# Half of a depthwise convolution as diagonal matmuls: a hybrid decoder layer on one core

## The chip, the cores and the metric

One core of a Trainium2 chip runs the whole layer in one launch. The metric is the device time of an execution in microseconds (us); the kernel before has a median of 936.02 us over 3 runs (934.52 to 939.70).

## What is computed

A decoder layer over 1024 tokens of width 1024, in float32. Three mixers read one projection of the normalised input: a gated linear attention (4 heads, chunks), a convolution module, and a causal differential attention (4 heads of 2 x 64). Their outputs are projected, added to x, and a mixture of 16 experts follows. The part that matters here, cut from the reference:

```python
def conv_mixer(u, w, b, gn_g, gn_b):
    a, gt = jnp.split(u, 2, axis=-1)
    z = a * jax.nn.sigmoid(gt)
    zp = jnp.pad(z, ((0, 0), (CONV_WIDTH - 1, 0), (0, 0)))          # CONV_WIDTH = 31
    y = lax.conv_general_dilated(zp, w[:, None, :], (1,), 'VALID',
                                 feature_group_count=CONV_CH) + b   # CONV_CH = 256
    ...                                                             # norm over groups of 64 channels
    return jax.nn.silu(yn)
```

Each of 256 channels is convolved along the tokens with its own 31 weights (taps), the present token and the 30 before it. The 256 channels are two halves of 128, which fill the partitions: ct = 0 and ct = 1.

## The kernel before

**Stages.** In order: norm of x and the projections of the linear attention (to about 97 us); the linear attention in two halves of 512 tokens (`gla_half`); 16 attention steps (4 heads by 4 pairs of token tiles); the output projection; the experts. The order on TensorE is the order of the program text. On VectorE, ScalarE, GpSimd and SyncE a scheduler orders the instructions by its own estimate of when each is ready; each engine then takes its queue strictly in that order.

**Three-pass matmuls.** Float32 operands are split into a high part, rounded to `fp32r`, and the rest (`split`: a copy on ScalarE, L129, and a subtraction on VectorE, L130). A product is the sum of three matmuls, high x high, high x low, low x high (`passes`).

**Filler.** `Filler` holds a queue of generators, each of which yields after every matmul it has issued. `F.fill(n)` lets them issue matmuls with n columns in all at that place in TensorE's order; `F.until(key)` runs the queue until a generator has ended. `gla_half` calls `fill` between the links of its chain: at `GLA_F[2]` to `GLA_F[5]` before and after the levels, `GLA_FILL` matmuls of 256 columns before each of the 7 levels, and `GLA_F[6 + hf]` behind the outputs. A level s (64, 32, ..., 1) is: `keys` on VectorE (L450, L451), the scores `pl` on TensorE (L460), and the scores' way into ST, by ScalarE copies (L469) for 64 and 32 and by two predicated copies on VectorE (L471) from 16 down. The score tiles in PSUM have two buffers, so a level's `pl` waits for the copies of the level before. When ST is complete, `po` (L516, L520) gives the half's output, and ScalarE and VectorE norm it (L524 to L531).

**The convolution.** `conv_proj` (generator "cu", 384 matmuls at L260 with 256 columns) makes z for both halves, and is the filler of the linear attention. `conv_taps` then starts y on ScalarE (L583) and adds one tap per instruction on VectorE, over nearly all 1024 tokens at once (L586); each tap reads and writes y, so the 30 taps of a half follow each other. Two tables, `TAPS[ct]` and `NORMS[ct]`, say how many taps and how many parts of `conv_norm` the program text has in each of the 16 attention steps, both with a priority that lets the scheduler bring them forward to where z is ready.

**Attention.** `head_proj` projects two token tiles per step (L251, 384 columns), brings q, k, v out (`vv`, L129 and L130; `qkr`, `qkss`, L663 to L671), and transposes them (`ptq`, L678). `head_attn` makes scores (L711), maxima (L718), exponentials (L720), transposes and outputs.

## Time and profile before

| | before |
|---|---|
| median of 3 runs | 936.02 us (934.52 to 939.70) |
| profiled execution: its own time / its span | 940.18 us / 938.6 us |
| TensorE matmul busy | 818.2 us (87%), 5256 instructions |
| VectorE busy | 649.2 us (69%), 1441 |
| ScalarE busy | 493.7 us (53%), 1094 |
| GpSimd busy | 165.0 us (18%), 165 |
| mean clock granted to TensorE | 0.931 |

The span runs from the first to the last instruction; the execution's own time is a little longer. In the profile PE is TensorE's matmuls, PEld its weight loads, DVE VectorE, ACT ScalarE. Matmuls are pipelined, so that a matmul's duration is longer than the distance to the next one. A `<-` behind idle time names what ended the wait. The granted clock is in shares of full speed: 1.00 is 2.4 GHz, 0.50 is 1.2 GHz, and a value between is a mean over both. One call of a float32 matmul counts twice in the trace (32 `pl` records are 16 calls).

### The profile page before, as it was taken

What the parts mean: (1) busy time and instruction counts of PE and PEld (TensorE: products, weight loads), DVE (VectorE), ACT (ScalarE), POOL (GpSimd) and SP (SyncE); (2) the same over time, 40 slices, a digit from 0 to 9 for tenths busy, and PEclk for the clock granted to TensorE, in tenths of its full rate; (3) what the DMA queues carried; (4) which work ended last, traced back from release to release, by engine and by line L of the source; (5) the groups of instructions that cost most, each with busy time, mean ns of one, the idle gap of its engine ahead of it and who ended that gap; (6) DMA issues with size and microseconds to landing.
All of it is one profiled execution on the core that took longest, in us unless ns stands there. A gap on an engine that the chain in (4) does not pass through costs nothing. (4 is left out here: it accounts for less than half of the span.)

```text
span 938.6 us, 14319 instructions
## 1 busy us (share of the span) xinstructions
PE 818.2 (87%) x5256; PEld 717.1 (76%) x5256; DVE 649.2 (69%) x1441; ACT 493.7 (53%) x1094; POOL 165.0 (18%) x165
## 2 busy tenths in 40 slices
PE   5999999789768998899878899999399999999870
PEld 4999989688658987788767688888278888888750
DVE  6841556988997666768857666666868677687850
ACT  6743516124246565667757554232558667677730
POOL 5100000000000000000000000000537666664221
PEclk9999989669879999999988999999689999999995
DMA  8210101102002002001202218434479999998942
GB/s 261 76 44 2 46 1 28 37 1 63 6 0 69 1 1 68 1 1 41 68 22 59 81 68 348 168 151 187 170 275 344 335 358 305 363 328 273 318 69 45
DMA packets 46007, 119.29 MB, mean 127 GB/s; under 512 B 6670, under 2 KB 26220, under 8 KB 38636
## 3 DMA queue, kind: packets, MB, share of 16 engines
q0 software_dynamic: 13104, 71.31, 23.0%
q1 hardware_dynamic: 28876, 41.15, 13.2%
q10 hardware_dynamic: 3952, 5.86, 1.7%
q8 instruction: 43, 0.70, 0.3%
q14 instruction: 32, 0.26, 0.1%
HBM read 97.33 MB, written 20.97 MB: 126 GB/s over the span
## 5 line engine op out<-in xcount | busy, mean ns | idle before, releaser
L1272 PE MATMUL pgu<-mw,xT 128*128 128x512 f32 x552 | 140.9, 404 | 0.8 <-ACT xT L129 0.8
L130 DVE TENSOR_TENSOR mw<-mraw,mw 128x1024 fp32r<-128x1024 f32 x99 | 120.9, 1256 | 11.3 <-ACT mw L129 10.4
L1272 PEld LDWEIGHTS pgu<-mw,xT 128*128 128x128 f32 x552 | 102.8, 190 | 24.9 <-issue 1.2
L129 ACT ACTIVATE mw<-mraw 128x1024 fp32r<-128x1024 f32 x113 | 112.9, 1052 | 14.4 <-PE pgu L1272 14.4
L251 PE MATMUL psA<-wh,hnh 128*128 128x384 f32 (+1 forms) x320 | 110.2, 344 | 1.0 <-ACT wh L129 1.0
L251 PE MATMUL psA<-wh,hnl 128*128 128x384 f32 (+1 forms) x320 | 110.6, 346 | 0.2 <-DVE xra L110 0.2
L251 PE MATMUL psA<-wl,hnh 128*128 128x384 f32 (+1 forms) x320 | 109.7, 343 | 0.9 <-DVE wl L130 0.9
L881 PE MATMUL psO<-woh,mx 128*128 128x512 f32 (+1 forms) x272 | 86.8, 396 | 3.5 <-DVE mx L130 2.5
L586 DVE SCALAR_TENSOR_TENSOR mix<-mix,par 128x994 f32<-128x994 f32 (+29 forms) x60 | 75.7, 1262 | 2.1 <-ACT mix L583 1.3
L942 POOL IOTA iota<- 128x128 f32 x1 | 0.2, 238 | 434.9 <-DVE mix L614 434.9
L1300 PE MATMUL py<-mw,hT 128*128 128x512 f32 x276 | 67.3, 392 | 4.5 <-DVE y L1304 2.9
L1300 PEld LDWEIGHTS py<-mw,hT 128*128 128x128 f32 x276 | 51.7, 188 | 16.7 <-ACT hT L129 3.9
L251 PEld LDWEIGHTS psA<-wh,hnh 128*128 128x128 f32 x320 | 63.2, 198 | 1.6 <-ACT wh L129 1.3
L251 PEld LDWEIGHTS psA<-wl,hnh 128*128 128x128 f32 x320 | 63.2, 197 | 1.3 <-DVE wl L130 1.2
L251 PEld LDWEIGHTS psA<-wh,hnl 128*128 128x128 f32 x320 | 63.1, 197 | 0.6 <-DVE hnl L130 0.4
L718 DVE TENSOR_REDUCE nm<-sc 128x1 f32<-128x128 f32 (+7 forms) x64 | 46.8, 751 | 21.7 <-PE sc L714 17.8
L720 ACT ACTIVATE e<-sc,nm 128x128 f32<-128x128 f32 (+7 forms) x64 | 47.3, 740 | 25.6 <-DVE nm L718 21.8
L881 PEld LDWEIGHTS psO<-woh,mx 128*128 128x128 f32 x272 | 49.8, 192 | 12.9 <-DVE mx L130 2.9
L260 PE MATMUL psA<-hnh,wl 128*128 128x256 f32 x192 | 57.1, 297 | 0.0
L260 PE MATMUL psA<-hnl,wh 128*128 128x256 f32 x192 | 57.0, 297 | 0.0
L260 PE MATMUL psA<-hnh,wh 128*128 128x256 f32 x192 | 56.1, 292 | 0.2 <-DVE mix L556 0.2
L881 PE MATMUL psO<-wol,mx 128*128 128x512 f32 (+1 forms) x136 | 53.5, 394 | 0.0
(388 smaller groups left out, 1841.8 us busy)
## 6 DMA issues: line engine op xcount, KB each, us to landing
mraw<-in_expert_w_gate_dram POOLq DMA_DIRECT2D x15, 1024.0 KB, 9.1
mraw<-in_expert_w_up_dram POOLq DMA_DIRECT2D x15, 1024.0 KB, 10.2
mraw<-in_expert_w_down_dram POOLq DMA_DIRECT2D x15, 1024.0 KB, 15.2
wraw<-in_w_in_dram SPq DMA_DIRECT2D x64, 128.0 KB
mix<-in_x_dram SPq DMA_DIRECT2D x8, 512.0 KB
wraw<-in_w_out_dram SPq DMA_DIRECT2D x16, 256.0 KB
h<-in_x_dram SPq DMA_DIRECT2D x8, 512.0 KB
out_dram<-h SPq DMA_DIRECT2D x8, 512.0 KB
```

The costliest lines, as they stand in the source:

```text
L129: K.nc.scalar.activation(hi, src, AF.Copy)
L130: (eng or K.nc.vector).tensor_tensor(lo, src, hi.bitcast(FT), op=OP.subtract)
L251: nc.tensor.matmul(ps[:, :n], a[:, k, cs], b[:, k % 2, :n], start=(k == 0 and t == 0), stop=(k == KT - 1 and t == 2))
L260: nc.tensor.matmul(ps, a[:, k % 2, c0:c0 + 128], b[:, k, :], start=(k == 0 and t == 0), stop=(k == KT - 1 and t == 2))
L586: nc.vector.scalar_tensor_tensor(y[:, sh:], z[:, :S - sh], w(t), y[:, sh:], op0=OP.mult, op1=OP.add)
L718: nc.vector.tensor_reduce(nm, scs[m][:, :n], axis=AX.X, op=OP.max, negate=True)
L720: nc.scalar.activation(e[:, :n], scs[m][:, :n], AF.Exp, bias=nm, accum_out=sums[:, u, m:m + 1])
L881: nc.tensor.matmul(ps, a[:, k, :], b[:, k % 4, c0 % 512:c0 % 512 + c1 - c0], start=(k == 0 and t == 0), stop=(k == KT - 1 and t == 2))
L942: g.iota(t, allow_small_or_imprecise_dtypes=True, **kw)
L1272: nc.tensor.matmul(ps, a[:, k, :], b[:, k % 4].rearrange("p a f -> p (a f)"), start=(n == 0), stop=(n == 23))
L1300: nc.tensor.matmul(py[:, c * 512:(c + 1) * 512], a[:, k, :], b[:, k, c * 512:(c + 1) * 512], start=(k == 0 and t == 0), stop=(k == 1 and t ...
```

## The change

The first channel half (ct = 0) leaves `conv_taps`. A new generator `conv_mm`, queued as "cv" behind "cu", computes it on TensorE: for each of the 31 taps a 128 x 128 matrix with the channels' weights on its diagonal, against z shifted by the tap, summed in one PSUM tile per column half of 512 tokens. With the three passes these are 31 x 3 x 2 = 186 matmuls of 512 columns (`pcv`, L616 of the new file). The diagonals (`dg`) are made on ScalarE from the identity with a scale per partition (L614): a high and a low one per tap and column half, 124 in all, with three buffers each. z is split once per column half (`dz`), with one buffer each. The fills of `gla_half` are made larger, and `F.until("cv")` ends the generator before the attention. `TAPS[0]` becomes empty, `TAPS[1]` and `NORMS[0]` are spread over other steps, and the pool of the norm's gain row is closed early, to give its room to the new tiles.

```diff
-GLA_FILL = 6
+GLA_FILL = 16
...
-TAPS = [[6, 6, 6, 6, 4, 2, 0, 0, 0, 0, 0, 0, 0, 0, 0, 0], [0, 0, 0, 0, 4, 4, 5, 5, 5, 4, 3, 0, 0, 0, 0, 0]]
-NORMS = [[0, 0, 0, 0, 0, 0, 0, 2, 0, 1, 1, 0, 0, 0, 0, 0], [0, 0, 0, 0, 0, 0, 0, 0, 0, 0, 0, 1, 2, 1, 0, 0]]
+TAPS = [[0] * 16, [3] * 10 + [0] * 6]
+NORMS = [[0, 0, 1, 0, 1, 0, 1, 1, 0, 0, 0, 0, 0, 0, 0, 0], [0, 0, 0, 0, 0, 0, 0, 0, 0, 0, 0, 1, 2, 1, 0, 0]]
...
-GLA_F = [40, 32, 16, 12, 10, 10, 44, 102]
+GLA_F = [40, 32, 24, 20, 16, 16, 60, 150]
...
+def conv_mm(K, dp, ct):
+    nc = K.nc
+    W = 31
+    y, z = K.mix[:, 2 + ct, :], K.z[:, ct, :]
+    wh = dp.tile([128, W], FT, name="dwh")
+    wr = dp.tile([128, W], FR, name="dwr")
+    wl = dp.tile([128, W], FT, name="dwl")
+    wv = K.par[:, R_CW:R_CW + 2 * W].rearrange("p (t c) -> p t c", c=2)[:, :, ct]
+    nc.scalar.activation(wr, wv, AF.Copy)
+    nc.scalar.activation(wh, wr.bitcast(FT), AF.Copy)
+    nc.vector.tensor_tensor(wl, wv, wh, op=OP.subtract)
+    for hf in range(2):
+        zs = [dp.tile([128, W - 1 + 512], FR, name=f"dz{x}") for x in range(2)]
+        lo = hf * 512 - (W - 1)
+        if hf == 0:
+            for t in zs:
+                nc.scalar.activation(t[:, :W - 1], K.ident[:, :W - 1], AF.Copy, scale=0.0)
+            split(K, zs[0][:, W - 1:], zs[1][:, W - 1:], z[:, :512])
+        else:
+            split(K, zs[0], zs[1], z[:, lo:lo + W - 1 + 512])
+        ps = K.psum.tile([128, 512], FT, name="pcv", tag="acc", bufs=2)
+        for t in range(W):
+            d = [dp.tile([128, 128], FR, name=f"dg{x}", bufs=3) for x in range(2)]
+            for x, wt in enumerate((wh, wl)):
+                nc.scalar.activation(d[x], K.ident, AF.Copy, scale=wt[:, t:t + 1])
+            for m, (a, b) in enumerate(passes(d, zs)):
+                nc.tensor.matmul(ps, a, b[:, t:t + 512], start=(t == 0 and m == 0), stop=(t == W - 1 and m == 2))
+                yield 512
+        nc.scalar.activation(y[:, hf * 512:hf * 512 + 512], ps, AF.Identity,
+                             bias=K.par[:, R_CBIAS + ct:R_CBIAS + ct + 1])
...
-    K.rowp = pool(K, sg, "rowp")
+    sr = ExitStack()
+    K.rowp = pool(K, sr, "rowp")
...
+    sr.close()
+    dp = pool(K, sg, "convd")
     F.add("cu", conv_proj(K, cp))
+    F.add("cv", conv_mm(K, dp, 0))
...
     gla_half(K, gp, 1, st, F)
+    F.until("cv")
     sg.close()
...
-    F.until("cu")
-    conv = [conv_taps(K, cp, ct) for ct in range(2)]
+    conv = [iter(()), conv_taps(K, cp, 1)]
```

**How the order moves.** VectorE in the last levels of the linear attention's second half, before (the taps, L586, are those of ct = 0; `lm_980` and `lm_986` are levels 2 and 1):

```order
L451 TENSOR_TENSOR kq<-mix,dex 128x256
L586 SCALAR_TENSOR_TENSOR mix<-mix,par 128x1001
L586 SCALAR_TENSOR_TENSOR mix<-mix,par 128x1002
L471 COPY_PREDICATED ST<-lm_980,pl 128x256x2
L586 SCALAR_TENSOR_TENSOR mix<-mix,par 128x1003
L471 COPY_PREDICATED ST<-lm_980,pl 128x256x2
L586 SCALAR_TENSOR_TENSOR mix<-mix,par 128x1004
L586 SCALAR_TENSOR_TENSOR mix<-mix,par 128x1005
L586 SCALAR_TENSOR_TENSOR mix<-mix,par 128x1006
L586 SCALAR_TENSOR_TENSOR mix<-mix,par 128x1007
L586 SCALAR_TENSOR_TENSOR mix<-mix,par 128x1008
L471 COPY_PREDICATED ST<-lm_986,pl 128x512 x2
```

The same place in the changed kernel; the taps are now those of ct = 1:

```order
L450 TENSOR_TENSOR kq<-mix,dex 128x256
L451 TENSOR_TENSOR kq<-mix,dex 128x256
L586 SCALAR_TENSOR_TENSOR mix<-mix,par 128x994
L586 SCALAR_TENSOR_TENSOR mix<-mix,par 128x995
L586 SCALAR_TENSOR_TENSOR mix<-mix,par 128x996
L471 COPY_PREDICATED ST<-lm_980,pl 128x256x2 x2
L586 SCALAR_TENSOR_TENSOR mix<-mix,par 128x997
L586 SCALAR_TENSOR_TENSOR mix<-mix,par 128x998
L586 SCALAR_TENSOR_TENSOR mix<-mix,par 128x999
L471 COPY_PREDICATED ST<-lm_986,pl 128x512
L586 SCALAR_TENSOR_TENSOR mix<-mix,par 128x1000
L471 COPY_PREDICATED ST<-lm_986,pl 128x512
```

Fifteen taps of ct = 0 stood ahead of the last copy into ST, the first of them behind the copies of level 16; now seven of ct = 1 stand there, the first behind the copies of level 4.

TensorE in the changed kernel around level 4 of that half (`pl` are a level's scores, `pcv` the new matmuls; before, the filler at each of these places was six matmuls of `conv_proj`):

```order
L460 MATMUL pl<-kq 128x64 x16
L414 MATMUL pdec<-gU,mix 128x128 x4
L616 MATMUL pcv<-dz_2275,dg_2283 128x512
L616 MATMUL pcv<-dz_2275,dg_2319 128x512
L616 MATMUL pcv<-dz_2276,dg_2319 128x512
L616 MATMUL pcv<-dz_2275,dg_2320 128x512
L616 MATMUL pcv<-dz_2275,dg_2326 128x512
L616 MATMUL pcv<-dz_2276,dg_2326 128x512
L616 MATMUL pcv<-dz_2275,dg_2327 128x512
L616 MATMUL pcv<-dz_2275,dg_2333 128x512
L460 MATMUL pl<-kq 128x64 x16
```

From here on the new matmuls take the place of `conv_proj`'s, which has ended by then; 26 of them stand ahead of the last `po`, 75 and 85 behind it.

VectorE where the first head's projection begins, before (`vv`, `qkss` and `qka` are the first head's; the taps are those of ct = 1):

```order
L586 SCALAR_TENSOR_TENSOR mix<-mix,par 128x1000
L130 TENSOR_TENSOR vv<-psA,vv 128x128
L586 SCALAR_TENSOR_TENSOR mix<-mix,par 128x1001
L667 TENSOR_REDUCE qkss<-qksq 128x4
L586 SCALAR_TENSOR_TENSOR mix<-mix,par 128x1002
L107 TENSOR_SCALAR qkv<-qkss 128x8
```

The same place in the changed kernel (L699 is the former L667):

```order
L586 SCALAR_TENSOR_TENSOR mix<-mix,par 128x1022
L586 SCALAR_TENSOR_TENSOR mix<-mix,par 128x1023
L130 TENSOR_TENSOR vv<-psA,vv 128x128
L699 TENSOR_REDUCE qkss<-qksq 128x4
L130 TENSOR_TENSOR vv<-psA,vv 128x128
L699 TENSOR_REDUCE qkss<-qksq 128x4
L107 TENSOR_SCALAR qkv<-qkss 128x8
```

Before, the taps of ct = 1 alternated with the first head's operations; now the last of them stands ahead of the first `vv`.

## Rows read from the trace of the kernel before

**Rows 1.** The page's slices (40 equal ones): TensorE's granted clock in tenths.
```profile
PEclk9999989669879999999988999999689999999995
```

**Rows 2.** Windows: stretch, length; busy PE, PEld, DVE, ACT, POOL (count); clock; DMA; GB/s.
```profile
97.00:145.20 48.20, 45.54 (x498) 42.82 (x497) 27.98 (x48) 18.04 (x40) 0.00 (x0) 0.93 0.09 23
145.20:168.30 23.10, 23.04 (x275) 22.00 (x276) 15.23 (x28) 13.61 (x27) 0.00 (x0) 1.00 0.18 48
168.30:204.20 35.90, 26.39 (x175) 23.75 (x174) 35.10 (x35) 3.25 (x7) 0.00 (x0) 0.54 0.04 12
204.20:224.80 20.60, 20.60 (x169) 20.60 (x170) 16.41 (x22) 9.34 (x21) 0.00 (x0) 0.97 0.00 1
224.80:252.40 27.60, 19.28 (x102) 18.12 (x100) 25.66 (x35) 7.39 (x18) 0.00 (x0) 0.88 0.22 58
252.40:286.70 34.30, 25.91 (x153) 22.65 (x152) 31.46 (x71) 14.73 (x50) 0.00 (x0) 0.85 0.00 1
...
329.50:355.00 25.50, 23.42 (x161) 20.77 (x160) 16.14 (x54) 15.82 (x54) 0.00 (x0) 1.00 0.01 2
```

**Rows 3.** The same windows, line 586 (the taps) alone: VectorE's busy time.
```profile
168.30:204.20 35.90, 27.31 (x22) 0.54 0.04 12
...
224.80:252.40 27.60, 19.81 (x16) 0.88 0.22 58
252.40:286.70 34.30, 18.06 (x15) 0.85 0.00 1
```

**Rows 4.** Waits of TensorE, 97 to 290 us: total us, times, longest.
```profile
PE pl L460 <- DVE ST L471: 8.4, 6, 2.0
...
PE ptq L678 <- DVE qkr L671: 6.4, 1, 6.4
PE po L516 <- DVE ST L471: 3.0, 1, 3.0
```

**Rows 5.** Timeline of TensorE, 729.8 to 734 us: start, us, instruction.
```profile
730.72 2.98 PE L1272 MATMUL pgu<-mw,xT 128*128 128x512 f32 x12
733.54 0.39 PE L1284 MATMUL pth<-ident,sg 128*128 128x128 f32 x2
```

**Rows 6.** Timeline of VectorE, 170 to 195 us: keys, three taps, two copies into ST.
```profile
172.74 0.42 DVE L450 TENSOR_TENSOR kq<-mix,dex 128x256 f32<-128x256 f32 x1
...
173.41 3.84 DVE L586 SCALAR_TENSOR_TENSOR mix<-mix,par 128x997 f32<-128x997 f32 x3
...
192.34 2.43 DVE L471 COPY_PREDICATED ST<-lm,pl 128x512 f32<-128x512 int32 x2
194.56 1.24 DVE L586 SCALAR_TENSOR_TENSOR mix<-mix,par 128x1009 f32<-128x1009 f32 x1
```

**Rows 7.** Timeline of TensorE: a level's scores and the outputs, first half and second half.
```profile
109.07 1.12 PE L460 MATMUL pl<-kq 32*128 32x64 f32 x32
...
134.20 1.00 PE L520 MATMUL po<-mix,ST 128*128 128x64 f32 x8
...
135.53 1.00 PE L520 MATMUL po<-mix,ST 128*128 128x64 f32 x8
...
171.12 2.57 PE L460 MATMUL pl<-kq 32*128 32x64 f32 x32 [1.99 <-DVE ST L471]
...
194.69 1.81 PE L520 MATMUL po<-mix,ST 128*128 128x64 f32 x8
...
197.25 1.81 PE L520 MATMUL po<-mix,ST 128*128 128x64 f32 x8
```

**Rows 8.** Timelines of ScalarE and VectorE: the split of a 512-column operand.
```profile
157.24 0.62 ACT L129 ACTIVATE wh<-wraw 128x512 fp32r<-128x512 f32 x1
...
158.59 0.68 DVE L130 TENSOR_TENSOR wl<-wraw,wh 128x512 fp32r<-128x512 f32 x1
```

**Rows 9.** ScalarE with a scale per partition, 128 columns: durations of L806, and a pair.
```profile
L806 ACT ACTIVATE on<-on,osa x32: 385/394/435, 279.8 to 567.4; 128x128 f32<-128x128 f32 x32
...
316.09 0.70 ACT L806 ACTIVATE on<-on,osa 128x128 f32<-128x128 f32 x2 [0.62 <-DVE osa L803]
```

## The prediction

> **What bounds the kernel now.** I read the page's slices first. The clock granted to TensorE falls to six tenths in the eighth and ninth of the 40 slices (164 to 211 us) and to eight and seven in the eleventh and twelfth (235 to 282) [rows 1]: the second half of the linear attention, and the entry of the attention. The windows cut this part into stages [rows 2]. The first half of the linear attention (97 to 145.2) and the start of the second (to 168.3) are TensorE's: busy 23.04 of 23.10 us at full clock. Then, from 168.3 to 204.2, VectorE is busy 35.10 of 35.90 us, TensorE only 26.39, at a mean clock of 0.54. At the entry of the attention it is the same: VectorE 25.66 of 27.60 and 31.46 of 34.30 us, TensorE 19.28 and 25.91.
>
> The same windows for line 586 alone say why: 22 taps of the convolution, 27.31 us, lie in the 35.9 us stretch, 16 and 15 in the two after it [rows 3]. The waits name the price on TensorE: 8.4 us of `pl` and 3.0 us of `po` behind VectorE's writes of ST, 6.4 us of a transpose behind `qkr` [rows 4]. So taps that sit in VectorE's queue between links of the chains for TensorE cost TensorE's time; TensorE is the bound elsewhere in these stages.
>
> **The change, part by part.** The sum is made on TensorE's queue from 97 us to the scores of the third attention step (286.7 us), since behind it no tap is left and the work is the same.
>
> *Taken away: TensorE's waits in the linear attention.* 8.4 + 3.0 = 11.4 us [rows 4].
>
> *Taken away: the half clock there.* A mean clock of 0.54 over 35.9 us is 33 us at half rate. TensorE was idle about 9.5 us of that stretch, so some 24 us of work ran at half rate and cost 12. The clocks of 0.93 over 48.2 us and 0.97 over 20.6 us add 2.4 and 0.6 [rows 2]. Together 15.0 us.
>
> *Taken away: the taps at the entry of the attention.* In the new order all 30 taps of the second channel half stand ahead of the first `vv`. They run while TensorE works off the rest of the diagonal matmuls, 160 of them, some 38 us, and 23 x 1.28 us of taps fit into that. The stretch of the first two steps, 34.3 us, should then be like that of the first two steps of the second head, 25.5 us at clock 1.00 [rows 2]: 8.8 us. The stretch before it, 27.6 us, holds 19.28 us of TensorE work at clock 0.88; without half rate this is about 17.5 us, and nothing waits for long: 10.1 us. Together 18.9 us. In sum 11.4 + 15.0 + 18.9 = 45.3 us go.
>
> *Added: 186 matmuls with 512 columns* (31 taps, 3 passes, 2 halves). Twelve such matmuls start at 730.72 and what follows at 733.54, so one takes 2.82 / 12 = 0.235 us [rows 5]: 43.7 us. The Trainium skill (TensorE: Matmul & The Clock Gate, section "Wait — 56ns, not 53.3ns?") gives 215.7 ns from start to start for 512 columns at full clock. By it the sum would be 3.6 us lower; the trace here shows 0.235, and I stay with that.
>
> The fills are larger too, but move conv_proj's 384 matmuls only forward; that costs nothing, because the count on TensorE's queue is the same. They are used up before the last levels of the second half. There the filler is 26 of the new matmuls, and 160 are left behind `po`.
>
> *Added: a new wait in the last levels.* The diff says the taps leave VectorE, but only the first half's do. The order shows the other half's taps moving up into their place: 3 before the write of ST for level 2, 3 before that for level 1 and one between its two parts, where 15 stood before. From the write of level 4 VectorE needs: keys 0.67 us, 3 taps 3.84, ST 2.22, 3 taps 3.84, then ST 2.22 with a tap of 1.24 in it, together 14.0 us [rows 6]. TensorE has in that time two score groups of 1.12 us [rows 7] and 16 new matmuls of 0.235: 6.0 us. So it waits about 8.0 us.
>
> *Added: half clock behind that wait.* Before, a wait of 1.99 us was followed by scores that took 2.57 us for 1.12, and the outputs `po` then took 2.56 us per group where the first half's took 1.33 [rows 7]. I take half rate for the four groups of `po`: 4 x 1.23 = 4.9 us. The bounds are nothing, and twice that if the diagonal matmuls behind also begin at half rate.
>
> *Added: the seam between the two column halves.* The pieces of z exist once, so the second half's split waits for the first half's last matmul, behind the evacuation on ScalarE: two operations on 512 columns there at 0.62 us, then one of 0.68 us on VectorE [rows 8], and I add 0.5 us for the ends between the three engines: 2.4 us. Between nothing and 5 if the clock falls.
>
> *Added on ScalarE: 124 diagonals.* The nearest row is a 128 x 128 activation with a scale per row: two in 0.70 us, 0.394 for one, so the second starts 0.31 us after the first [rows 9]. A tap takes 0.62 us of ScalarE and 0.705 of TensorE, and three buffers run ahead, so TensorE stays the bound and the price is nothing. The upper end is 0.394 with no overlap: 0.79 us a tap, 53 taps x 0.08 = 4.5 us, and with ScalarE's other work in that tail (on, two mix, two evacuations, a split: some 5.5 us) about 10 us. The three first pairs of diagonals, ahead of 97 us, lie where ScalarE waits for TensorE.
>
> *Moved:* the norms of the first half come at steps 2 to 7 instead of 7 to 10, same count: nothing, as VectorE has room there (16.14 of 25.5 us) [rows 2]. The loads on SyncE keep their order; the weight splits of the first head now stand before the tail.
>
> **The sum:** 43.7 + 8.0 + 4.9 + 2.4 - 45.3 = +13.7 us on the profiled execution of 940.18 us. That one is 4.2 us above the median of the runs, 936.0; on the median I forecast **950 us**, slower by 1.5%. By itself this case reaches from 944 to 956.
>
> **Rivals.**
> *1. ScalarE bounds the tail.* For it: 106 diagonals follow each other there, each waiting for a buffer that TensorE frees. Against it: the pair in 0.70 us. It decides from 0.35 us a diagonal; price 10 us, with a clock that falls in the small gaps up to 16: 960 to 966 us.
>
> *2. The clock comes back during `po`.* In the first half `po` went from half to full rate within one burst (its later groups 1.33 us); in the second half 10 us of it stayed at half [rows 7]. If the new matmuls before it keep the rate up, 4.9 us fall away: 945 us. The Trainium skill (TensorE: Matmul & The Clock Gate, "What's actually happening") speaks for this: half rate is the resting state and sustained activity releases it. The second half's `po` here did not follow that.
>
> *3. The last levels are not held, the other side.* If the taps run in the shadow of TensorE's own work, the 8.0 and 4.9 us are not paid: +0.8 us, 937. The place is the pair of writes of ST at levels 2 and 1; the point is 1.6 us of new waits in all (45.3 - 43.7): under it the kernel is faster. With no seam and 512 / 2.4 GHz = 0.213 us a matmul (39.7 us), 39.7 - 45.3 = -5.6: 930 us. Against it: VectorE takes its queue in order, and 14.0 us of work cannot hide behind 6.0.
>
> *4. The change doesn't relieve the attention's entry.* If the taps of the second half are still running when the first head's `vv` come, up to 18.9 us stay: 969 us. Against it: the tail is as long as the taps.
>
> **How the numbers follow.** The forecast 0.45, rival 1 0.18, rival 2 0.14, rival 3 0.19, rival 4 0.04. Range 934 to 966: it leaves out rival 4 and the far end of rival 3. Of this kernel a measurement can tell about 0.5%, 4.7 us, from no change. Faster by more is half of rival 3: 0.10. Within 0.5%: the other half of it, with the lower edges of the forecast and of rival 2: 0.17. Slower: 0.73.
>
> **What would show it.** Right: about 186 matmuls `pcv` at 0.235 us with TensorE near full in a tail of some 42 us between `po` and the first attention projection; waits of `pl` and `po` behind ST of some 8 us in the second half; no wait of a transpose behind `qkr`; the third step's scores some 14 us later than 286.7. Wrong: `pcv` waiting for ScalarE (rival 1), a clock near 1 in the second half's `po` (2), no waits behind ST there (3), taps beside the first head (4). If the scores of the third step come at 287 or earlier, the sum has failed on the side of the gains.

## The result, and the profile after

The changed kernel takes 943.84 us (median of 15 runs, 941.19 to 948.67). Beside it the kernel before took 939.7 us (15 runs). The ratio is 1.0051, with a 95% interval of 1.0033 to 1.007: slower by 0.5%, some 4 us, where the forecast had +13.7 and 1.5%. The direction was right, the size was not. The forecast's 950 also stood on the median of three runs, 936.0; on 939.7 the same sum would have been 953.4.

The profiled execution took 948.67 us (span 947.0), 8.4 us more in span than the one of before. The slices of the page, against [rows 1]: of the low clock in the sixth, eighth, ninth, eleventh and twelfth slices only eight tenths in the ninth are left; behind that it's there about as before, in the 23rd slice (seven tenths) instead of the 22nd, and in the 29th and 30th (seven and seven instead of six and eight).

```profile
PEclk9999999989999999999989799999779999999995
```

The windows of the same stages (columns as in [rows 2]):

```profile
96.50:145.20 48.70, 48.47 (x550) 46.39 (x549) 27.00 (x47) 20.77 (x45) 0.00 (x0) 1.00 0.14 37
145.20:169.10 23.90, 23.56 (x193) 22.99 (x191) 14.07 (x24) 11.09 (x25) 0.00 (x0) 1.00 0.13 34
169.10:210.10 41.00, 36.14 (x392) 31.65 (x392) 30.84 (x41) 17.71 (x40) 0.00 (x0) 0.92 0.16 40
210.10:252.50 42.40, 40.28 (x169) 31.83 (x169) 28.35 (x28) 36.95 (x108) 0.00 (x0) 0.96 0.00 1
252.50:295.08 42.58, 40.56 (x256) 37.14 (x255) 21.07 (x70) 19.64 (x66) 0.00 (x0) 1.00 0.00 1
```

The third line is the second half of the linear attention, the fourth the tail of diagonal matmuls (42.4 us, forecast 42), the fifth the attention's entry. The entry takes 42.6 us where the last two stretches before it took 61.9 [rows 2]. The third step's scores start at 295.08, 8.35 us later than before.

The new wait, in TensorE's timeline (start, us, instruction, idle time before it and what ended it):

```profile
191.06 0.44 PE L460 MATMUL pl<-kq 32*128 32x64 f32 x4 [0.83 <-DVE ST L471]
...
197.25 0.44 PE L460 MATMUL pl<-kq 32*128 32x64 f32 x4 [2.45 <-DVE ST L471]
198.39 1.97 PE L460 MATMUL pl<-kq 32*128 32x64 f32 x28 [0.69 <-DVE ST L471]
200.29 3.78 PE L616 MATMUL pcv<-dz,dg 128*128 128x512 f32 x8
203.87 1.04 PE L516 MATMUL po<-stlast,qb 128*128 128x256 f32 x2
...
205.45 0.66 PE L520 MATMUL po<-mix,ST 128*128 128x64 f32 x4 [0.15 <-DVE ST L471]
```

and VectorE's queue that makes it:

```profile
190.30 1.29 DVE L471 COPY_PREDICATED ST<-lm,pl 128x512 f32<-128x512 int32 x2
...
192.16 3.83 DVE L586 SCALAR_TENSOR_TENSOR mix<-mix,par 128x994 f32<-128x994 f32 x3
195.91 2.42 DVE L471 COPY_PREDICATED ST<-lm,pl 128x512 f32<-128x512 int32 x2
198.13 3.82 DVE L586 SCALAR_TENSOR_TENSOR mix<-mix,par 128x997 f32<-128x997 f32 x3
...
204.10 1.29 DVE L471 COPY_PREDICATED ST<-lm,pl 128x512 f32<-128x512 int32 x1
```

This is the forecast's chain: 190.30 to 205.39, 15.1 us (forecast 14.0). TensorE's waits on ST in it are 4.3 us, not 8.0, because its work was slowed meanwhile: the last scores take 1.97 for 1.12, eight `pcv` 3.78 for 1.9. Waits and slow work together are 7.1 us. Then `po` came back to full rate: a group of it takes 2.08 us at first, then 1.32.

The diagonal matmuls and their diagonals, by line:

```profile
L616 PE MATMUL pcv<-dz,dg x186: 387/395/795, 184.8 to 252.2; 128*128 128x512 f32 x186
L614 ACT ACTIVATE dg<-ident,dwh x62: 384/402/405, 71.7 to 250.4; 128x128 fp32r<-128x128 f32 x62
```

From 232.62 the last 85 take 19.8 us to the next instruction: 0.233 us each, against 0.235 in [rows 5]. The second line is the high diagonals; the 62 low ones (`dwl`) run beside them. ScalarE waits 10.7 us for TensorE to free diagonals, 7.8 of it ahead of the tail. In the tail it is busy 18.0 of 19 us (233 to 252), so it keeps up with little to spare; that it doesn't set the pace is shown by e3 below.

### The profile page after: what moved, and what is told of

It is laid out like the page before. It is cut to its first block, busy times and chain, and to the rows that moved or that the text cites. A ratio compares the mean times of both kernels' runs of the same rounds, so it can differ in the third digit from the quotient of the medians.

```text
span 947.0 us, 14847 instructions
## 1 busy us (share of the span) xinstructions
PE 849.0 (90%) x5442; PEld 740.8 (78%) x5442; DVE 620.5 (66%) x1414; ACT 535.2 (57%) x1225; POOL 162.3 (17%) x165
## 5 line engine op out<-in xcount | busy, mean ns | idle before, releaser
L1332 PE MATMUL py<-mw,hT 128*128 128x512 f32 x276 | 68.9, 399 | 3.5 <-DVE y L1336 2.2
L260 PE MATMUL psA<-hnh,wl 128*128 128x256 f32 x192 | 55.0, 286 | 0.0
L260 PE MATMUL psA<-hnl,wh 128*128 128x256 f32 x192 | 54.6, 285 | 0.0
L616 PE MATMUL pcv<-dz,dg 128*128 128x512 f32 x186 | 48.7, 418 | 2.7 <-ACT dz L129 1.4
```

Source lines behind the costliest of these rows:

```text
L260: nc.tensor.matmul(ps, a[:, k % 2, c0:c0 + 128], b[:, k, :], start=(k == 0 and t == 0), stop=(k == KT - 1 and t == 2))
L616: nc.tensor.matmul(ps, a, b[:, t:t + 512], start=(t == 0 and m == 0), stop=(t == W - 1 and m == 2))
L1332: nc.tensor.matmul(py[:, c * 512:(c + 1) * 512], a[:, k, :], b[:, k, c * 512:(c + 1) * 512], start=(k == 0 and t == 0), stop=(k == 1 and t ...
```

## The experiments

All times in one table. "Scores" is the start of the third step's scores in the profile, "to projection" the time from there until the fourth head is ready for its first output projection, "mx" TensorE's waits in that projection. The last four columns come from the timelines of each profile, so from one execution each; the first two from all runs of the comparison. The three profiles of the changed kernel differ by 5.0 us in "scores" and 2.2 in "to projection": smaller differences in these columns show little by themselves.

| kernel | median us (runs) | ratio to before, interval | scores | to projection | mx | span |
|---|---|---|---|---|---|---|
| before | 939.7 (15) | | 286.7 | 229.1 | 3.5 | 938.6 |
| before, again | 940.54 (1) | | 287.6 | 228.4 | 3.4 | 938.9 |
| changed | 943.84 (15) | 1.0051, 1.0033 to 1.007 | 295.1 | 223.0 | 7.7 | 947.0 |
| changed, again | 945.87 (6) | 1.0049, 1.0025 to 1.0072 | 300.0 | 222.0 | 7.3 | 946.2 |
| changed, third | 948.78 (1) | | 296.5 | 220.8 | 7.4 | 947.1 |
| e1: gate | 942.61 (12) | 1.0014, 0.9984 to 1.0044 | 292.8 | 222.8 | 7.4 | 942.3 |
| e10: filler | 947.16 (12) | 1.0087, 1.0057 to 1.0117 | 297.7 | 220.4 | 5.0 | 944.4 |
| e11: gate, filler | 938.31 (10) | 0.9982, 0.9959 to 1.0005 | 290.4 | 220.6 | 8.3 | 938.7 |
| e13: gate, late | 944.48 (12) | 1.0037, 1.0012 to 1.0063 | 295.5 | 218.8 | 7.7 | 942.2 |
| e3: two passes | 939.1 (10) | 0.9983, 0.9962 to 1.0004 | 294.8 | 221.2 | 2.9 | 937.2 |
| e5: before, fills | 943.07 (10) | 1.0035, 1.001 to 1.0061 | 290.6 | 225.6 | 3.1 | 942.6 |
| e8: before, gate | 935.15 (10) | 0.9957, 0.9932 to 0.9981 | 283.3 | 227.3 | 2.8 | 933.6 |
| e15: norms back | 947.9 (10) | 1.0077, 1.0042 to 1.0111 | 293.0 | 225.4 | 7.8 | 945.7 |
| e16: weights | 933.37 (7) | 0.9929, 0.9891 to 0.9966 | 300.8 | 220.7 | 1.0 | 937.1 |
| e18: before, weights | 931.77 (7) | 0.9919, 0.9887 to 0.9951 | 287.9 | 226.4 | 0.5 | 928.3 |
| e14: split | 929.36 (6) | 0.989, 0.9851 to 0.9929 | 284.5 | 225.8 | 2.7 | 930.1 |
| e17: split, norms | 923.62 (6) | 0.9821, 0.9782 to 0.9861 | 280.6 | 218.8 | 2.7 | 917.6 |
| e19: all | 915.87 (6) | 0.977, 0.9728 to 0.9812 | 279.7 | 218.5 | 0.5 | 909.5 |

### More profiles of the two kernels

No edit.

> The changed kernel as it is, for a second profile. The first one had a span of 947.0 us, 8.4 longer than the kernel before, where the medians differ by 4.1; behind the third step's scores the two traces take the same 651.9 us. Theory A (the four outputs po are not slowed by the clock in this kernel, and the rest of what the forecast missed is the spread of single executions): again po in about 6.2 us at full rate behind waits of the scores on VectorE of some 3 to 4 us, third step's scores at 295 give or take 1, and a span between 940 and 948 that goes with the granted clock behind them. Theory B (the profile caught po in a lucky phase): po takes some 10 us at half rate in this one, and the third step's scores come at 299.

> The kernel before as it is, for a second profile. In the first one the third step's scores start at 286.7 and what follows takes 651.9 us; the changed kernel's two profiles have 295.1 and 300.1, and 651.9 and 646.2 behind. Theory A (the part behind the third step varies by some 6 us from one execution to the next in both kernels alike, with the clock in the attention's fourth head and at the first experts): third step's scores again at 286 to 288, and between 645 and 653 us behind them. Theory B (the part behind is shorter in the changed kernel by its own doing, and that is why the medians differ by 4 while the stage differs by 8 to 13): again about 652 behind.

> The changed kernel as it is, for a third profile. Theory A: the third step's scores between 295 and 300, by the clock in po of the second half (full or half rate), and between 645 and 652 us behind them. Theory B (the part behind is shorter in the changed kernel by its own doing): about 646 behind; 651.9 in the first profile was the exception.

In the second profile `po` of the second half runs at half rate after waits of 4.0 us, so the scores come at 300.0; in the third it comes back to full rate in its first group, 296.5. In the second profile `po` takes 10.8 us where it took 6.0 (203.9 to 209.9) in the first, and TensorE's timeline shows where the waits fell, with the window behind it:

```profile
199.38 1.11 PE L460 MATMUL pl<-kq 32*128 32x64 f32 x28 [0.44 <-DVE ST L471]
...
204.20 0.70 PE L516 MATMUL po<-stlast,qb 128*128 128x256 f32 x2 [1.65 <-DVE ST L471]
...
206.43 1.12 PE L520 MATMUL po<-mix,ST 128*128 128x64 f32 x4 [1.14 <-DVE ST L471]
```

```profile
204.20:215.20 11.00, 9.86 (x41) 9.13 (x42) 9.52 (x8) 0.00 (x0) 0.00 (x0) 0.57 0.00 0
```

So both cases of the forecast's clock term occur in one and the same program. They differ in where TensorE waits for VectorE: in the first profile the last scores ran slowly (1.97 us), TensorE came to `po` late and waited 0.15 us there; in the second they ran at full rate (1.11), TensorE came early, waited 2.8 us at `po` itself, and half rate followed. In the third it waited nothing there. The other profiles say the same: wherever TensorE waited 1.1 us or more at the second half's `po` (both of before, e3, e4, e5, e10, e16, e18), its later groups took 2.2 to 2.6 us (in e5 1.9, then 1.3), and wherever it waited under 0.5 us, they took 1.3. Behind the scores 651.9, 646.2 and 650.6 us follow, against 651.9 and 651.3 before: neither theory, but a sum of two things that differ in the table, "to projection" and "mx".

### The last levels: gate and filler

e1 keeps every tap behind the last copy into ST; e10 has no gate, but more filler ahead of the last levels; e11 has both; e13 gates and spreads `conv_proj` so that it lasts until `po`.

```diff
+                K.gla_st = nc.vector.copy_predicated(...).ins
...
-                    if GATE and ct == 0:
-                        with tc.issue_after(K.gla_last):
+                    if ct == 1:
+                        with tc.issue_after(K.gla_st):
```

```diff
-        F.fill(GLA_FILL * 256)
+        F.fill((GLA_FILL if hf == 0 or li < 5 else [28, 36][li - 5]) * 256)
...
-    F.fill(GLA_F[5] * 256)
+    F.fill((GLA_F[5] if hf == 0 else 40) * 256)
```

e11 has [24, 28] and 24 there. e13 has 6 a level and GLA_F of before in the first half, and 16, 16, 20, 24, 32, 36, 36 and 32 in the second.

> The second channel half's taps on VectorE all stand behind the last write of ST, so none lies between the links of the last levels; otherwise the changed kernel. Theory A (the taps ahead of the writes of ST at levels 2 and 1 hold the scores, and the half clock follows from that): the stretch from level 4's scores to po, 16.6 us in the changed kernel, takes 7.8 us; the 30 taps run beside the diagonal matmuls behind po (30 x 1.28 = 38 us from about 196, so they end at 239 to 241, just before the attention starts at about 244): 8.8 us less, 935 us, faster than both kernels. Rival B (what the levels gain the attention's entry gives back, since the taps now end too late): vv and qkr wait, the entry takes over 42.6 us, 940 to 944. Rival C (the half clock there comes from something else than the wait): scores still take 1.97 us for 1.12, and only the waits of 3.4 us go: 940.

> The changed kernel with 32 of its 186 diagonal matmuls in place of 24 as filler between the last levels and po: 14, 18 and 20 ahead of level 2, level 1 and po of the second half, where 8 each stood, so 28 fewer are left behind po; nothing else moves. Theory A (the waits behind ST at levels 2 and 1 cost twice, by themselves and by the half clock that follows; filler costs nothing, since it only moves): the waits on ST of 4.3 us in the first profile and 4.0 in the second go, and with them the half clock from level 1 to po, 2.8 us in the first and some 8 in the second: third step's scores at 287 to 289 instead of 295 and 300, 944 - 7 = 937 or less. Rival B (the clock falls there without any wait, as it did in the kernel with the taps gated, where 1.5 us of waits were left): scores still take 1.97 us for 1.12, only the waits go, third step's scores at 292, 940. Rival C (what is gained ahead of the third step is lost behind it, as between the first two profiles of the changed kernel): third step's scores at 288, but 944 all the same.

> The kernel whose second half's taps stand behind the last write of ST, with 12, 14 and 12 diagonal matmuls as filler ahead of level 2, level 1 and po of the second half, where 8 each stood. Theory A (1.5 us of waits at level 2 bring the half clock there, and filler takes both away): no wait on ST over 0.3 us, level 1's scores in 1.12 us, third step's scores at 287 to 289 instead of 292.8, about 937. Rival B (the clock falls without a wait): scores at 1.6 to 1.97 us again, third step's scores at 291.5, 941.

> The kernel whose second half's taps stand behind the last write of ST, with the fills of the first half as before the change (6 a level), and those of the second half's levels larger (16 to 36 units of 256 columns), so that conv_proj's matmuls last until po and all 186 diagonal matmuls stand behind po. Theory A (the diagonals come late from ScalarE at levels 4 to 1, 0.6 to 1.9 us of waits of pcv there, and with the waits behind ST they bring the half clock; conv_proj's matmuls need no diagonals): no wait over 0.3 us between 168 and po, scores in 1.12 us, po at full rate, the 186 in 43.7 us with the seam: third step's scores at 284 to 287 instead of 290.4 of the gated kernel with more filler, about 933. Rival B (the clock falls in the last levels without a wait): scores of levels 2 and 1 at 1.6 to 1.97 us, 938. Rival C (the taps end too late: 30 x 1.28 = 38 us from about 203, with conv_proj's writes and the weight splits between them to 245 or later, as the tail ends): waits at vv and qkr, 940.

*e1*: the waits on ST fall to 1.0 us, but level 2 and the `pcv` behind it still run at half rate and level 1 partly: rival C's clock, and only 2.3 us of the 8.8 show in this one profile. The taps, ending at 244, cost the entry nothing (42.6 us), against rival B. *e10* (14, 18 and 20 matmuls are 52 in place of 24; the 32 in its text is a slip) is slower than the changed kernel. VectorE's queue there:

```profile
192.79 5.12 DVE L586 SCALAR_TENSOR_TENSOR mix<-mix,par 128x994 f32<-128x994 f32 x4
197.83 2.46 DVE L471 COPY_PREDICATED ST<-lm,pl 128x512 f32<-128x512 int32 x2
200.09 7.72 DVE L586 SCALAR_TENSOR_TENSOR mix<-mix,par 128x998 f32<-128x998 f32 x6
207.72 2.43 DVE L471 COPY_PREDICATED ST<-lm,pl 128x512 f32<-128x512 int32 x2
```

The room that the filler makes is taken by more taps, 4 and 6 instead of 3 and 3: the last copy ends at 210.2, `po` waits 2.7 us and runs at half rate. None of my three theories had that. *e11*, with the gate as well, has no wait on ST and gains 5.5 us on the changed kernel; its scores come at 290.4. What is left are 1.9 us of waits for diagonals and half rate behind them. *e13* has no such wait and no half rate from 166 to 203.7 (clock 1.00), yet its scores come at 295.5: its first half, with the small fills, runs at 0.95 over 68.9 us with waits again, and 186 matmuls in one piece take 49.2 us with seam and waits. Filler is moved, not made.

### The price and the gain by themselves

e3 leaves out the third pass, e4 the whole convolution of the first channel half but one tap.

```diff
-            for m, (a, b) in enumerate(passes(d, zs)):
+            for m, (a, b) in enumerate(passes(d, zs)[:2]):
```

```diff
 def conv_mm(K, dp, ct):
...
+    nc.scalar.activation(y, z, AF.Identity, scale=w, bias=...)
+    return
+    yield
```

> Leaves out one of the three passes of the diagonal matmuls (the low part of the weights, so 124 matmuls instead of 186; both diagonals per tap are still written). Theory A (TensorE bounds the tail and the price of the change is 0.235 us a matmul): up to 62 x 0.235 = 14.6 us less, 929 us, but only as long as ScalarE keeps up. Theory B (ScalarE's two diagonals at 0.30 us each are right under TensorE's three passes at 0.70): a tap falls from 0.70 to 0.60 us and no further, 53 x 0.10 + 9 x 0.235 = 7.4 us less, 936.5, with pcv waiting for the diagonals all through the tail. Theory C (ScalarE bounds the tail already in the changed kernel): no change, 944.

> Leaves out the first channel half's convolution but for one tap, which is one operation on ScalarE: no diagonals, no diagonal matmuls, so what taking the taps off VectorE is worth without the price on TensorE. Theory A (the gain is about 40 to 45 us, and the diagonal matmuls cost their full count): 160 matmuls behind the last levels x 0.235 = 37.6 and the seam of 2.1 go, 904 us; the filler of the last levels ran beside waits and gives nothing. Rival B (the tail of diagonal matmuls is also the cover of the second half's taps: without it some 20 taps, 26 us, stand ahead of the first vv): 8 to 19 us come back at the attention's entry, 912 to 923, with vv or qkr waited for there. Rival C (the taps of the first half cost little before): less than 25 us under the changed kernel, 919 or more, and no wait at the attention's entry.

*e3*: the scores come at 294.8, no earlier than with all 186. In it the low diagonals are still written, but nothing reads them, so no buffer holds them back: all 62 are done by about 102 us, and in the tail ScalarE writes one diagonal per tap.

```profile
L614 ACT ACTIVATE dg<-ident,dwl x62: 386/390/400, 73.4 to 102.2; 128x128 fp32r<-128x128 f32 x62
```

So theory B, two diagonals per tap as the limit, isn't put to the test here. Behind `po` the first nine `pcv` start about 0.43 us apart at a low clock, then they follow each other at 0.233 us:

```profile
222.00:226.20 4.20, 4.20 (x12) 3.33 (x12) 3.05 (x4) 2.63 (x5) 0.00 (x0) 0.55 0.00 0
226.30:232.20 5.90, 5.90 (x26) 4.52 (x24) 3.62 (x8) 5.23 (x15) 0.00 (x0) 1.00 0.00 0
```

That is the pace of the changed kernel's tail too, with two diagonals per tap: TensorE sets it, not ScalarE. From the end of `po` to the attention e3 takes 30.2 us instead of 42.6, as theory A's price has it (62 x 0.233 = 14.4, less what half rate took of it). But ahead of that TensorE waits longer (10 us, for diagonals and for ST), as twelve taps stand ahead of the last copy into ST instead of seven, and `po` runs at half rate: what the tail gains is lost there. The median's 5 us come from behind: `mx` is waited for 2.9 us instead of 7.4. *e4*: without a convolution the routing is another (576 matmuls `pgu` instead of 552), so its 948.03 us say nothing and only the stage counts: scores at 274.2, 21 to 26 us earlier than with the 186, not 40. The waits of TensorE there, from its timeline:

```profile
207.87 1.22 PE L516 MATMUL po<-stlast,qb 128*128 128x256 f32 x2 [5.44 <-DVE ST L471]
229.12 1.94 PE L537 MATMUL pt<-ident,ong 128*128 128x128 f32 x8 [10.74 <-DVE ong L531]
```

Rival B, at another place than it said: not the attention but the gate output `ong` stands behind the taps. With `pl` TensorE waits 25.3 us there for VectorE, against 4.3 in the first profile of the changed kernel. So the diagonal matmuls (43 us) partly run in time that TensorE would have waited, and taking the taps off VectorE, in this order and with the larger fills, is worth 13 us (287.2 to 274.2).

### The kernel before with one part of the change

e5 has the larger fills alone, e8 the gate alone (both channel halves).

```diff
-GLA_FILL = 6
+GLA_FILL = 16
...
-GLA_F = [40, 32, 16, 12, 10, 10, 44, 102]
+GLA_F = [40, 32, 24, 20, 16, 16, 60, 150]
```

> The kernel before with the larger fills of the change alone: 60 taps on VectorE, no diagonal matmuls. Theory A (the fills alone give nothing; conv_proj's matmuls run out ahead of the last levels, where the waits on ST then have no filler at all): waits of pl and po behind ST of 15 us or more instead of 11.4, third step's scores at 288 to 292, 940 to 945. Rival B (earlier filler is worth something by itself, as the first half's waits go): third step's scores at 283, 936.

> The kernel before with all 60 taps behind the last write of ST: nothing leaves VectorE, the taps only move out of the last levels. Theory A (VectorE bounds this whole part: 92.2 of 97.8 us busy from 168 to 266 in the kernel before; what the levels gain, the entry of the attention loses): no waits on ST, po some 15 us earlier, then waits of the attention's transposes on qkr or vv of 10 us and more, third step's scores at 284 to 290, 938 to 943. Rival B (the waits and the half clock at the levels were the whole loss, and moving the taps is enough): third step's scores at 272 to 278, 928, and the diagonal matmuls not needed.

*e5* follows theory A: waits of 17.1 us of `pl` and 5.4 of `po` behind ST. *e8* is the surprise: nothing leaves VectorE, the taps only wait for the last copy, and the kernel is 0.4% faster than before. TensorE's waits from 168 to 284 us, longest last:

```profile
PE ptq L678 <- DVE qkr L671: 10.1, 1, 10.1
PE pa L739 <- DVE e L726: 9.4, 3, 4.9
...
PE pl L460 <- DVE ST L471: 1.2, 2, 0.7
```

Against [rows 4], `po` has none left and `pl` little, and `qkr` 10.1 instead of 6.4: theory A's exchange, a little better than even.

### Behind the third step

VectorE in the changed kernel at the fourth head, and ScalarE (ACTq is its queue):

```profile
515.84 1.76 ACTq L874 DMA_DIRECT2D wr<-in_router_expert_w_dram  x1
```

```profile
523.44 0.36 DVE L875 TENSOR_TENSOR wr<-wr,par 128x192 f32<-128x192 f32 x1 [4.30 <-DMA wr<-in_router_expert_w_dram]
...
525.25 1.22 DVE L130 TENSOR_TENSOR mx<-mix,mx 128x1024 fp32r<-128x1024 f32 x1
```

```profile
526.53 0.79 PE L913 MATMUL psO<-woh,mx 128*128 128x512 f32 x1 [5.56 <-DVE mx L130]
```

VectorE waits 4.30 us for the router weights, which nobody needs yet, with `mx` behind them in its queue, and TensorE waits 5.56 for `mx`. In the kernel before the issue took 0.60 us and the same place reads:

```profile
513.54 0.60 ACTq L842 DMA_DIRECT2D wr<-in_router_expert_w_dram  x1
```

```profile
520.01 1.22 PE L881 MATMUL psO<-woh,mx 128*128 128x512 f32 x2 [2.50 <-DVE mx L130]
```

e15 puts the table of the first half's norms back; e16 and e18 issue the two loads of the router weights from GpSimd, in the changed kernel and in the kernel before. VectorE's scaling of them then stands behind both parts of `mx`.

```diff
-NORMS = [[0, 0, 1, 0, 1, 0, 1, 1, 0, ...
+NORMS = [[0, 0, 0, 0, 0, 0, 0, 2, 0, 1, 1, ...
```

```diff
-    nc.scalar.dma_start(wr[:, :, :4], ...
+    nc.gpsimd.dma_start(wr[:, :, :4], ...
...
-    nc.scalar.dma_start(wr[:, :, 8:], ...
+    nc.gpsimd.dma_start(wr[:, :, 8:], ...
```

> The changed kernel with the first half's norms at the steps at which they stood before the change (7, 9 and 10 instead of 2 to 7). Theory A (the early norms are worth 6 us behind the third step, which the forecast took for nothing; VectorE and ScalarE have room at steps 2 to 7 only since the taps are gone): from the third step's scores to the output projection of the fourth head some 228 us instead of 222, third step's scores 1 us earlier as one norm matmul stands ahead of them, 949. Rival B (that stretch is shorter for another reason, no tap or write of the convolution reaching into it): 222 us again, 944.

> The changed kernel with the two loads of the router weights issued by GpSimd, whose queue is idle there, instead of ScalarE; VectorE's scaling of them then stands behind the two parts of mx in its order. Theory A (VectorE waits 3.6 to 4.3 us for these weights with mx behind them in its queue, and TensorE for mx): the waits of the first output projection fall from 7.4 to 3 us or less, 940, which is what the kernel before takes. Rival B (the wait only hides another one, or is a thing of profiled executions, which lie 4 us above the median of this kernel): the profile shows no such wait, but the median stays at 943 to 945.

> The kernel before with the two loads of the router weights issued by GpSimd instead of ScalarE, as in e16_wr. The stretch of the fourth head's first output projection took 30.8 us in the kernel before, 36.4 in the changed kernel and 27.2 in the changed kernel with this edit. Theory A (the change made this wait worse by 4 us of waits and 2 of half clock, the rest was there before): 27 us here as well, 3 to 4 us less, 936, so that the changed kernel with the edit, 933.4, is about equal to it or a little faster. Rival B (the kernel before gains as much as the changed one): 930, and the change stays 4 us slower. Rival C (the wait there covered something else): no gain, 939.5.

*e15*: 225.4 us to the projection instead of 220.8 to 223.0, and a median 4 us higher than the changed kernel's: theory A in direction, some 3.5 us of the 6, though against the kernel before the two intervals (1.0042 to 1.0111 and 1.0033 to 1.007) overlap. *e16* gains 10.5 us, more than theory A had. The windows from the moment when the fourth head is ready to its last scores, for the changed kernel, e16, before and e18 (those of e16 and e18 begin 0.5 and 1.2 us late; up to the end of the last scores the four stretches take 36.8, 28.0, 31.2 and 27.4 us):

```profile
518.10:554.50 36.40, 27.89 (x147) 21.66 (x148) 21.05 (x46) 17.48 (x43) 0.00 (x0) 0.86 0.24 72
```

```profile
522.00:549.20 27.20, 25.28 (x148) 19.64 (x148) 20.70 (x46) 16.40 (x43) 0.00 (x0) 1.00 0.29 100
```

```profile
515.80:546.60 30.80, 26.51 (x147) 20.65 (x148) 20.80 (x45) 16.47 (x40) 0.00 (x0) 0.94 0.23 84
```

```profile
515.50:542.70 27.20, 25.92 (x152) 20.27 (x152) 20.00 (x52) 15.58 (x44) 0.00 (x0) 1.00 0.27 94
```

With the wait the half clock goes too (0.86 and 0.94 become 1.00): the stretch is 8.8 us shorter in the changed kernel and 3.8 before. But e18's median falls by 8.5 us, rival B's gain rather than A's. The wait doesn't explain all of it: e18's profile is 10.4 us shorter than the two of before, of which 3.9 lie in this stretch, 4.9 behind it and 1.7 ahead of it; e16's, too, gains 3.9 behind it. Why is not shown. With this wait out of both, the changed kernel stands at 933.37 and the kernel before at 931.77, and their intervals overlap: no difference that these runs can tell, where rival B had 4 us.

### A version that beats both

Of the first channel half, 512 columns become 93 diagonal matmuls, the other 512 stay taps; all taps behind the last copy into ST, fills of before but for the last, which stays 150 (e14). e17 adds the early norms, e19 the router weights on GpSimd.

```diff
-    for hf in range(2):
+    for hf in range(1):
...
+        a = max(512 if ct == 0 else 0, sh)
-        nc.vector.scalar_tensor_tensor(y[:, sh:], z[:, :S - sh], w(t), y[:, sh:], ...
+        nc.vector.scalar_tensor_tensor(y[:, a:], z[:, a - sh:S - sh], w(t), y[:, a:], ...
```

> The kernel before with all taps behind the last write of ST (third step's scores there at 283.3), and of the first channel half only the first 512 columns as diagonal matmuls: 93 instead of 186, behind po and conv_proj, no seam; the other 512 columns stay 30 taps on VectorE. Fills as before the change. Theory A (with the levels free, VectorE bounds that kernel and TensorE the gated kernel with all 186, whose scores came at 290.4, so dividing the convolution between them is better than either): VectorE's work falls by 30 x 0.6 = 18 us, TensorE has 93 x 0.235 = 21.9 us less than with 186: third step's scores between 268 and 276, 923 to 932, faster than both kernels. Rival B (what remains of the taps, 58 us, still collides with the attention's entry, where the transposes wait for qkr): third step's scores at 280 to 285, 935. Rival C (what is gained here is lost behind the third step by the clock): 935 or more with scores at 276 or earlier.

> The fastest version so far (one column half of the first channel half as 93 diagonal matmuls, all taps behind the last write of ST; 929.4) with the first half's norms early, at steps 2 to 7. Theory A (early norms are worth 5 to 6 us): from the third step's scores to the output projection 220 to 222 us instead of 225.8, 924 to 926. Rival B (here taps still run at steps 0 to 2, so that early norms wait or press on the attention's entry): third step's scores 2 to 4 us later than 284.5, 928 to 931.

> One column half of the first channel half as diagonal matmuls, all taps behind the last write of ST, early norms (923.6), and the router weights loaded by GpSimd. Its waits for mx are 1.7 us so far, as ScalarE's issue of that load takes 0.60 us there. Theory A (that wait goes, with some half clock): 1 to 3 us less, 921 to 922.5. Rival B (it hides behind the other): 923.5.

e14 took 929.36 us, in theory A's range, but not by its path: its scores come at 284.5, where rival B had them (`qkr` 3.6 us). Its profile gains on e8's behind the third step, 645.6 against 650.3 us. Of that 3.2 us lie behind the fourth head's last scores, a part that takes 388.9 to 393.2 us in the three profiles of the changed kernel alone, so single executions differ by as much; more isn't shown. e17 gains 5.7 us, and its stretch to the projection is 218.8 us for 225.8, as expected (its profile, 917.6, is one of its shortest runs). e19 takes 915.87 us, 2.3% under the kernel before and 3% under the changed one; it gains more than the 1 to 3 us expected, as e16 and e18 did.

## Why the prediction was right and wrong

*Right: the mechanism of the stage.* The first half's waits and the entry's are gone, the tail has the forecast length, ScalarE keeps up, seven taps of the second channel half hold the last levels. The chain is 15.1 us against 14.0, the waits and slow work in it 7.1 us against 8.0, the seam 2.1 against 2.4. The price of a matmul was 0.233 us, against the row's 0.235. The Trainium skill (TensorE: Matmul & The Clock Gate, section "Wait — 56ns, not 53.3ns?") gives 0.2157, which this trace doesn't reach. In the three profiles the scores come 7.9, 12.9 and 9.4 us later than the 287.2 of before (mean of two). The 13.7 of the sum is near the second of these.

*Wrong, first: "half clock behind that wait", 4.9 us.* In `po` it is there in one of three profiles (10.8 us instead of 6.0). I took the wait of 8.0 us and half rate in `po` as two prices, paid one after the other. The profiles show them as alternatives: where the half rate fell on the last scores and the `pcv` ahead of `po`, it ran inside the time that VectorE's chain takes anyway, TensorE hardly waited at `po`, and the rate came back in `po`'s first group; only where TensorE waited at `po` itself did `po` run at half rate. The outcome of rival 2 came in two of three, but not by its condition, as the `pcv` ahead of `po` had not kept the rate up there (eight took 3.78 us instead of 1.9). The Trainium skill (TensorE: Matmul & The Clock Gate, section "What's actually happening") has it that sustained activity releases half rate. The trace agrees: in the first profile TensorE worked on from 198.4 us with one wait of 0.15, and `po`'s groups went from 2.08 to 1.32 us. The mean of the stage is therefore +10.0 and not 13.7.

*Wrong, second: "the norms of the first half: nothing".* The stretch to the fourth head's projection is 6.8 us shorter in the mean of the profiles (221.9 against 228.7). e15 gives back about half of it. That the other half is the norms' too is not shown: e5, which moves no norm, has 225.6 in this stretch. Room on VectorE at steps 2 to 7 was there, as I said; but I did not ask what the norms had cost at steps 7 to 10, where they stood.

*Wrong, third: "behind it no tap is left and the work is the same".* The same work waited longer: from the fourth head's being ready to its last scores, 36.2 us against 31.3 in the means, +4.9, with the late router weights (e16 takes it away). +10.0 - 6.8 + 4.9 is +8.1; the profiled spans differ by 8.0 (946.8 against 938.75).

*Open.* The medians differ by 4 to 5, not 8, so some 4 us of the miss have no cause that is shown. The three profiled executions of the changed kernel (947.8 to 948.8 us) lie above its median in the other runs; their granted clock is 0.952 to 0.955, where the mean of the 21 timed runs of the table's first two rows for it is 0.957. Less half clock, then, but in which stretch a run without a trace doesn't show. e16's scores at 300.8 with a span of 937.1, beside 300.0 and 946.2, show how far the stage and the total can part.

*The rivals.* Rival 1 (ScalarE) is refuted: the tail runs at 0.233 us a matmul with two diagonals per tap and with one (e3). Rival 3 was half right: the wait can be removed (e11, gate and filler together), and then the kernel is no slower than before; with the gate alone (e1) the interval holds 1 as well, so what the filler adds is shown by one profile only. Rival 4 didn't happen.

## What to carry to other kernels

Before work is moved to another engine, order the queue of the first: keeping the taps behind the last link of the chain gained some 4 us (0.4%) with nothing moved, and half of the first channel half on TensorE then gained more than the whole of it. Matmuls that run where TensorE would have waited cost less than their count: e4 and the changed kernel differ by 21 to 26 us, not by 43. And after a change compare every stretch up to the end, also those that it doesn't touch: equal remainders (651.9 and 651.9 here) can be a gain and a new wait of the same size.

## What the runs showed of the hardware

ScalarE's issue of the router weights took 1.4 to 2.1 us in each of the eight profiles with 186 diagonal matmuls and that load on its queue, and 0.60 in the others. In each of the eight a transfer of instructions on queue q8 lies in that issue; in none with 0.60 does one. In the first profile, the transfers from 515 to 516 us:

```profile
q8 instruction: 1, 0.02, 6.9%
```

In e16, with the weights on GpSimd, the stretched issue is the next one on ScalarE (1.68 us, a load that nobody waits for), and the transfer on q8 lies in it again. It is not ScalarE's own code by its spacing: in the first profile, from 25 to 908 us, 108 to 146 of TensorE's matmuls lie between one transfer on q8 and the next, and 3 to 87 of ScalarE's instructions, so it goes with TensorE's count. Why an issue of ScalarE takes longer beside it isn't shown. The Trainium skill (Runtime: NRT & Kernel Launch, section "Instruction fetch mechanics") says that an engine's instructions are streamed in blocks and that crossing one is mostly hidden. Here 1.2 us show, on another engine's queue. The weights then landed 7.6 us after the start of the issue instead of some 3.4. Two loads of 512 KB on the other queue had begun meanwhile (in the kernel before they began 1.2 us behind the end of the weights' issue), and from 518 to 519 us only that other queue moved anything: so it fits that a delay of 1.2 us became one of 4 by that, but no run shows it alone.

The clock of one and the same stretch differs between executions of one program, and a wait at its head goes with it: `po` took 6.0 and 6.2 us where TensorE waited 0.15 us and nothing there, and 10.8 where it waited 2.8.
